# A list scheduler of an FFN: transfer times from the trace, due times for PSUM copies, accumulators joined later, and the first plain down burst taken into the list

## Chip, core and metric

The kernel runs on one core of one Trainium2 chip. The metric is device time in microseconds: the median of three runs of the kernel before is 1355.8 us (1353.67 to 1356.29). Float32 goes in and comes out.

## What is computed

One layer of a hybrid decoder: sequence 1024, width 1024, FFN width 2816. The attention and short-convolution half comes first; the change touches the FFN half only.

```python
D_MODEL = 1024; SEQ = 1024; D_FF = 2816; FFN_CONV_K = 3
...
        merged = jax.nn.sigmoid(g_att) * y_att + jax.nn.sigmoid(g_conv) * y_conv
        x = x + rms_norm(merged @ w_out[l], norm_mix_post[l])

        h = rms_norm(x, norm_ffn_pre[l])
        u = causal_dwconv(h @ w_up[l], conv_ffn_w[l])
        a, g = jnp.split(u, 2, axis=-1)
        f = (jax.nn.gelu(g, approximate=True) * a) @ w_down[l]
        x = x + rms_norm(f, norm_ffn_post[l])
```

## The kernel before

Every float32 operand is scaled and split into two float16 halves, and three float16 products stand for one float32 product. The scale needs the operand's sum of squares: ACT squares and sums each tile (`jk_u`, `jk_dn`, `jk_f`), DVE reduces the sums and writes them as `rb_...`, a matmul of one column with ones (`pr_...`) totals them over the partitions, and DVE makes the scale (`sc_u`, `sp_dn`, `sp_f`). ACT then writes the high half and DVE the low one (`wh_u`, `wdh`, `f16`, and `fa`, `fy`, `fs`, `fx`, `wq` for the quads).

The FFN's 22 chunks of 128 rows (`f` = 0 to 21) come in groups of 4, 4, 4, 4, 3 and 3. A chunk has an up projection of seven products of 12 matmuls, a Strassen scheme over two 512-column halves, which go to three PSUM banks `pu{f}a`, `b` and `c` in the order a, b, c, a, b, c, b. After each product its bank is copied or added out: by ACT to `cg`, `ug` and `ca`, by DVE to `ca` and `cg`. Then come the convolution (`ua`, `ug`), the gelu and the product `ua`. The chunk's weights are two tiles of 512 KB (`ws_u{f}_0`, `_1`) that SP loads.

The first four groups go through the down projection as quads: seven Strassen products of four tiles each, 28 steps of 6 matmuls (`pq`). ACT copies each bank out, scaled, to `st`, and POOL sends every two copies by DMA to a DRAM accumulator `acc[i, e]`, 512 KB: a plain write for the first group, an accumulating DMA for the other three. Beside the last chunks the accumulators are joined (`join`): SP loads them to `yacc` and `u2`, POOL accumulates two more on top, and DVE adds `u2` to three halves of every `yacc` pair. The last two groups are plain: `down` multiplies the split `f16` and `wdh`, and DVE adds `pd` to `yacc`. For the fifth group this runs behind the list, and `dn_split` loads its `w_down` tiles and those of the sixth a second time (`wd`), because the list has only taken their sums of squares.

All up to the last chunk is given to a list scheduler, `Plan`. `add` notes a job with its engine, its cost in us, the tiles it reads and writes, how far it may run ahead of its latest start (`ahead`), and by when it should be done (`due`, reckoned on the clock of the PE jobs). PE products are a fixed sequence (`seq`); other jobs are taken by time and latest start, and a `pr` matmul is put in at once when the list has its operand ready. `order` counts buffers of the pools (16 slots of 4 KB per partition, 4 `ws`, 8 `wh`, 8 PSUM banks) and one DMA queue: a transfer starts when the last one ends. The jobs' code is then emitted in that order, which fixes each engine's instruction order; the chip's engines run these in order and wait on semaphores.

Lines: 1426 `load`, 1450 the `pr` matmul, 1462 and 1464 the two halves, 1537 the up products, 1543 to 1555 their copies, 1697 the quad matmuls, 1701 the `st` copies, 1727 the adds of `join`, 1333 the reloads, 1367 the plain down matmuls.

Of the kernel before, what the change touches and what calls it, by code (L numbers as in the profile page):

```python
# [40 lines left out]
class Layer:  # L41
# [1270 lines left out]
    def ffn(self):  # L1312
# [88 lines left out]
        C = dict(A=0.97, Ah=0.5, Aq=1.18, V=1.21, Vh=0.64, Vp=0.72)  # L1401
# [24 lines left out]
        def load(eng, b, dst, srcf, mb=1.3, r=(), w=None, **kw):  # L1426
            e = nc.sync if eng == "SP" else nc.gpsimd
            j = pl.add(eng, 0.45 if eng == "SP" else 1.1, lambda: e.dma_start(dst(), srcf(), **kw), r,  # L1428
                       [b] if w is None else w, ahead=1e9 if kw or r else AHEAD["load"])
# [187 lines left out]
        def w_sums(g):  # L1617
# [117 lines left out]

        ET = mybir.EngineType
        with tc.manual_schedule(engines={ET.PE, ET.DVE, ET.Activation, ET.SP, ET.Pool}):
# [4 lines left out]
            for f in range(NFF):  # L1742
                g = max(g for g in range(ng) if ff0[g] <= f)
                n = f - ff0[g]
                if f >= 2:
                    up_open(f)
                    up_prod(f, 1)
                if f >= 1 and not (n == 2 and 1 <= g <= NQ):
                    up_prod(f - 1, 4)
                    up_done(f - 1)  # L1750
                if n == 0 and 1 <= g <= NQ:
                    f_quads(g - 1)
                if n == 1 and g == NQ + 1:
                    f_plain(g - 1)
                up_prod(f, 6)
                if f >= 2:
                    up_prod(f, 5)
                    up_prod(f, 2)
                up_prod(f, 7)
                up_prod(f, 3)  # L1760
                if f + 3 < NFF:
                    up_weights(f + 3)
                if n == 1 and 1 <= g <= NQ:
                    quad_open(g - 1)
                    for k, i in enumerate((1, 2, 5, 3, 7, 4, 6)):
                        quad_prod(g - 1, i)
# [3 lines left out]
                if n == 1 and g < NQ:  # L1770
                    w_quads(g)
                if n == 1 and g >= NQ:
                    w_sums(g)
                if g == NQ and n == 2:
                    for tt in range(4):
                        join(tt)
# [2 lines left out]
        for g in (ng - 2,):
            f16[g] = [b.t for b in up[f"q{g}"].f]  # L1780
            invd[g] = fb[g].t["inv"]
        for g in (ng - 2, ng - 1):
            draw[g] = sqs[g].t
        fts[ng - 1] = [up[ff0[ng - 1] + n].ua.t for n in range(GROUPS[ng - 1] - 1)]
# [2 lines left out]
        p, pr = up[NFF - 1], prs[NFF - 1]
        pr.ca, pr.cg, pr.ug, pr.ps = p.ca.t, p.cg.t, p.ug.t, {"b": p.bank["b"].t}
        pr.ua = p.ua.t
        pr.inv = p.sb.t["inv"]  # L1790
        self.pw[f"u{NFF - 1}"] = [b.t for b in p.w], pr.inv
# [396 lines left out]
```

## Time and profile before

| | |
|---|---|
| median of 3 runs | 1355.8 us (1353.67 to 1356.29) |
| the profiled execution | 1353.56 us |
| its span, first to last instruction | 1351.8 us |
| granted TensorE clock, mean | 0.991 |
| bytes moved by DMA | 126.55 MB |

The page gives busy time for each engine over the span, then the span in 40 slices of 33.8 us. PE is the matmul row, PEld the loading of weights beside it, SPq the queue from which SP issues DMAs. In a row of the timeline stand start, length, engine, line, operation, what it writes and reads, how many were merged, and in brackets the idle time before it with what ended that. A row of the waits gives the waiting instruction, what it waited for, us in total, times, and the longest. Names in the profile leave the numbers of buffers out, so `pr_u` stands for `pr_u3` to `pr_u21`.

### The profile page before, as it was taken

To read this page: it belongs to the slowest core of one execution; us is meant where nothing else is said; L and a number is where in the kernel's file an instruction comes from. 1 tells how busy PE (TensorE), PEld (TensorE's weight loads), DVE (VectorE), ACT (ScalarE), POOL (GpSimd) and SP (SyncE) were. 2 spreads that over 40 slices of the span, in tenths; PEclk is the share of its full clock that TensorE was granted. 3 is DMA by queue.
4 is the path that set the end of the run, shared out by engine and by line. 5 is a ranking of instruction groups with operands and counts; after the bars stand their busy time and mean duration, and the time that the engine had idled before them with its cause. 6 is when DMAs were issued, how large, how long until landed. Compare 5 with 4: busy or idle time off the path is not lost.

```text
span 1351.8 us, 17009 instructions
## 1 busy us (share of the span) xinstructions
PE 1302.7 (96%) x6406; PEld 582.3 (43%) x6406; DVE 1095.4 (81%) x1761; ACT 942.0 (70%) x1338; POOL 85.7 (6%) x122
## 2 busy tenths in 40 slices
PE   8999999999999999999999999999899889969997
PEld 4444444444444444444544444444344334324443
DVE  6678988887889867887899999799499669748986
ACT  7578878887788947665576769777677766647625
POOL 2000000000000000000110001002100300130003
PEclk9999999999999999999999999999999999989999
DMA  7111111110112113422420315405911941697117
GB/s 267 33 33 47 48 32 32 48 32 17 47 32 73 39 61 109 157 77 94 145 73 32 125 32 211 162 32 101 241 63 32 213 129 33 137 286 200 57 37 125
DMA packets 36981, 126.55 MB, mean 94 GB/s; under 512 B 4241, under 2 KB 4369, under 8 KB 36898
## 3 DMA queue, kind: packets, MB, share of 16 engines
q1 hardware_dynamic: 26240, 88.76, 19.5%
q0 software_dynamic: 10656, 36.70, 13.0%
q8 instruction: 50, 0.82, 0.2%
q14 instruction: 33, 0.27, 0.1%
q10 hardware_dynamic: 2, 0.00, 0.0%
HBM read 87.67 MB, written 37.78 MB: 93 GB/s over the span
## 4 chain that ended last, share of the span: by engine, by line
PE 49%; issue 25%; DVE 11%; DMA 6%; ACT 5%; POOL 4%; POOLq 0%; DVEq 0%; SPq 0%; ACTq 0%
PE py L1180 5%; PE pcb L212 3%; PE pcc L212 3%; PE pcx L212 3%; PE pk L212 3%; PE pq L212 3%; PE pywa L806 3%; PE pywc L806 3%; DMA ws_u<-w_up_nt 3%; PE pd L1367 3%; POOL acc L1428 2%; PE A L834 2%; PE o L834 2%; PE z L834 2%; PE pv L407 1%
## 5 line engine op out<-in xcount | busy, mean ns | idle before, releaser
L1537 PEld LDWEIGHTS <-wh_u 128*128 128x128 f16 x1764 | 172.0, 98 | 216.2 <-issue 13.1
L1464 DVE SCALAR_TENSOR_TENSOR wh_u<-ws_u,sc_u,wh_u 128x1024 f16<-128x1024 f32 (+1 forms) x60 | 65.6, 1104 | 28.0 <-ACT wh_u L1462 27.7
L2058 PEld LDWEIGHTS <-wh_g 128*128 128x128 f16 x588 | 56.9, 98 | 69.0 <-issue 0.8
L1701 ACT ACTIVATE st<-pq,sd 128x512 f32<-128x512 f32 x112 | 70.0, 686 | 19.9 <-DVE ua L1582 13.3
L1180 PE MATMUL py<-wh_wo,m 128*128 128x512 f16 x384 | 83.7, 379 | 0.0
L877 ACT ACTIVATE sh<-sp 128x1024 f16<-128x1024 f32 (+3 forms) x48 | 40.5, 843 | 52.2 <-DVE sp L872 52.0
L1428 POOL DMA_DIRECT2D acc<-st x56 | 43.4, 774 | 466.9 <-ACT st L1701 466.9
L59 ACT ACTIVATE jk_u<-ws_u 128x1024 bf16<-128x1024 f32 x44 | 46.2, 1051 | 35.0 <-DMA ws_u<-w_up_nt 34.8
L1367 PE MATMUL pd<-wdh,f 128*128 128x512 f16 (+1 forms) x297 | 62.4, 372 | 0.6 <-ACT wdh L98 0.6
L1462 ACT ACTIVATE wh_u<-ws_u,sc_u 128x1024 f16<-128x1024 f32 (+1 forms) x60 | 59.3, 998 | 3.8 <-DVE sc_u L1447 3.5
L872 DVE TENSOR_TENSOR sp<-A,sp 1x1024 f32<-1x1024 f32 (+3 forms) x40 | 35.9, 897 | 29.8 <-PE A L834 26.5
L881 DVE TENSOR_TENSOR sh<-sp,sh 128x1024 f16<-128x1024 f32 (+3 forms) x48 | 45.8, 955 | 13.5 <-ACT sh L877 13.3
L1180 PEld LDWEIGHTS <-m 128*128 128x128 f16 x384 | 37.4, 98 | 44.2
L1571 DVE SCALAR_TENSOR_TENSOR ua<-ca,cw_a,ua 128x1023 f32<-128x1023 f32 (+1 forms) x40 | 51.1, 1278 | 1.1 <-ACT ua L1569 1.1
L907 DVE SCALAR_TENSOR_TENSOR w<-e,w 128x1024 f16<-128x1024 f32 (+3 forms) x48 | 45.8, 954 | 6.8 <-ACT w L903 6.7
L903 ACT ACTIVATE w<-e 128x1024 f16<-128x1024 f32 (+3 forms) x48 | 40.5, 844 | 14.7 <-DVE e L898 13.7
L1697 PE MATMUL pq<-wq,fs 128*128 128x512 f16 x192 | 44.6, 389 | 5.0 <-ACT st L1701 4.7
L1571 DVE SCALAR_TENSOR_TENSOR ug<-cg,cw_g,ug 128x1023 f32<-128x1023 f32 (+1 forms) x38 | 48.6, 1278 | 0.0
L898 DVE TENSOR_TENSOR e<-e,g 128x1024 f32<-128x1024 f32 (+3 forms) x48 | 45.7, 952 | 2.5 <-ACT g L894 2.5
L867 ACT ACTIVATE sp<-e,one 128x1024 f32<-128x1024 f32 (+3 forms) x48 | 44.4, 926 | 4.0 <-DVE e L862 2.7
L853 ACT ACTIVATE e<-z,cz 128x1024 f32<-128x1024 f32 (+3 forms) x48 | 43.1, 898 | 3.6 <-PE z L834 3.6
L212 PE MATMUL pcb<-hT,wh_cb 128*128 128x512 f16 x192 | 45.1, 380 | 0.0
(766 smaller groups left out, 3042.3 us busy)
## 6 DMA issues: line engine op xcount, KB each, us to landing
acc<-st POOLq DMA_DIRECT2D x56, 512.0 KB, 8.5
ws_u<-w_up_nt SPq DMA_DIRECT2D x44, 512.0 KB
ds<-w_down SPq DMA_DIRECT2D x22, 512.0 KB
ws_g<-w_in_nt SPq DMA_DIRECT2D x14, 512.0 KB
x<-x SPq DMA_DIRECT2D x8, 512.0 KB
ws_wo<-w_out SPq DMA_DIRECT2D x8, 512.0 KB
xr<-x SPq DMA_DIRECT2D x8, 512.0 KB
yacc<-acc SPq DMA_DIRECT2D x16, 256.0 KB
```

The lines of the kernel that those rows point to most:

```text
L212: nc.tensor.matmul(ps, w[:, wi, ds(k * P, P)], hT[:, hi, k, ds(c * NH, NH)], start=n == 0, stop=n == last)
L806: nc.tensor.matmul(ps, w[0][:, wi, ds((d % 2) * NH + k * P, P)], acts[bi][k][:, hi, ds(c * NH, NH)], start=n == 0, stop=n == 11)
L834: nc.tensor.matmul(out, w, mv, skip_group_check=True, **kw)
L1180: nc.tensor.matmul(ps, m16[k][:, hi, ds(tt * P, P)], wo[k][:, wi, sl], start=k == 0 and p == 0, stop=k == 7 and p == 2)
L1367: nc.tensor.matmul(pd[nh], f16[g][k][:, hi, ds(tt * P, P)], w[k][:, wi, ds(*part)], start=run is runs[0] and n == 0, stop=run is runs[-1] ...
L1428: j = pl.add(eng, 0.45 if eng == "SP" else 1.1, lambda: e.dma_start(dst(), srcf(), **kw), r, [b] if w is None else w, ahead=1e9 if kw or r ...
L1462: A(C["A" if big else "Ah"], lambda: act.activation(dst.t[:, 0, dsl], src.t[:, ssl], AF.Copy, scale=sb.t["s"]), [(src, sreg), sb], [(dst, ...
L1464: V(C["V" if big else "Vh"], lambda: vec.scalar_tensor_tensor(dst.t[:, 1, dsl], src.t[:, ssl], sb.t["s"], dst.t[:, 0, dsl], ALU.mult, ALU. ...
L1537: pe.matmul(b.t, p.w[wt].t[:, wi, ds(wc * NH + k * P, P)], pr.block(i, h, k), start=first and n == 0, stop=n == 3 * KH - 1, skip_group_che ...
L1571: V(C["V"], lambda lag=lag: vec.scalar_tensor_tensor(u.t[:, lag:], c.t[:, :T - lag], sm.t[:, 2 - lag:3 - lag], u.t[:, lag:], ALU.mult, ALU ...
L1701: A(C["Ah"], lambda tt=tt, b=b, st=st: act.activation(st.t[:, tt % 2, :], b.t, AF.Copy, scale=q.sd.t[:, 0:1]), [b, q.sd], [(st, str(tt % 2))])
L2058: nc.tensor.matmul(ps, w[wt][:, wi, ds(wc * NH + k * P, P)], self.block(i, hi, k), start=first and n == 0, stop=n == 3 * KH - 1, skip_grou ...
```

## The change

Seven things are edited, all in the FFN's list: the costs of ACT's split (`As`, `Ash`) get entries of their own; loads are reckoned longer, and start 1.9 us (SP) or 2.4 us (POOL) after their issue; accumulating DMAs count 2.7 us; the `st` copies and the down copies get a due time of 3 us behind their products; the loads of `join` may run only 20 us ahead of need, where they had no limit, and `u2` is loaded and accumulated for two tiles at once; the raw `w_down` tiles of the sixth group stay in `ws` buffers and are split in the list; and the first plain down burst (`down_plain`), with the end of the last chunk, is in the list too, in place of `dn_split`, `finish` and `down` behind it. The loop over the chunks becomes a generator (`steps`), whose option to interleave products (`inter`) is left at zero.

```diff
-        C = dict(A=0.97, Ah=0.5, Aq=1.18, V=1.21, Vh=0.64, Vp=0.72)
+        C = dict(A=0.97, Ah=0.5, As=1.04, Ash=0.6, Aq=1.18, V=1.21, Vh=0.64, Vp=0.72)
...
-        def load(eng, b, dst, srcf, mb=1.3, r=(), w=None, **kw):
+        def load(eng, b, dst, srcf, mb=1.45, r=(), w=None, ahead=None, **kw):
...
-            j = pl.add(eng, 0.45 if eng == "SP" else 1.1, lambda: e.dma_start(dst(), srcf(), **kw), r,
-                       [b] if w is None else w, ahead=1e9 if kw or r else AHEAD["load"])
+            j = pl.add(eng, 0.45 if eng == "SP" else 1.14, lambda: e.dma_start(dst(), srcf(), **kw), r,
+                       [b] if w is None else w, ahead=AHEAD["load"] if ahead is None else ahead)
...
-        AHEAD = dict(load=45.0, sq=40.0, up=32.0, quad=40.0, wq=60.0)
+        AHEAD = dict(load=45.0, sq=40.0, up=32.0, quad=40.0, wq=60.0, wp=40.0, join=20.0, pr=3.0, cv=1.0, ca=1.0, mb=2.7)
...
-        DUE = dict(conv=20.0, fin=25.0)
+        DUE = dict(conv=20.0, fin=25.0, ev=3.0)
...
-                b = slab(f"ds{ff0[g] + n}")
+                b = slab(f"ds{ff0[g] + n}") if g < ng - 1 else \
+                    Buf("ws", lambda n=n: self.ws.tile([P, D], F32, tag="ws", name=f"ds{ff0[g] + n}"))
...
-                  [b, q.sd], [(st, str(tt % 2))])
+                  [b, q.sd], [(st, str(tt % 2))], due=DUE["ev"])
...
-                    load("G", None, lambda e=tt // 2: acc[i, e], lambda st=st: st.t, r=[st], w=[accb[i, tt // 2]], mb=1.6, **kw)
+                    load("G", None, lambda e=tt // 2: acc[i, e], lambda st=st: st.t, r=[st], w=[accb[i, tt // 2]], mb=AHEAD["mb"], ahead=1e9, **kw)
...
-            u = slab(f"u2_{tt}", [P, NH])
+            if tt % 2 == 0:
+                us[tt // 2] = slab(f"u2_{tt}", [P, 2, NH])
+            u = us[tt // 2]
...
-                load(eng, None, lambda: b.t[:, sl], lambda: m(i), r=[accb[i, tt // 2]], w=[(b, reg)], mb=0.65, **kw)
-            ld("SP", u, slice(0, NH), None, 1)
+                load(eng, None, lambda: b.t[:, sl], lambda: m(i), r=[accb[i, tt // 2]], w=[(b, reg)], mb=1.35 if kw else 0.72, ahead=AHEAD["join"], **kw)
+            if tt % 2 == 0:
+                load("SP", u, lambda: u.t, lambda: acc[1, tt // 2], r=[accb[1, tt // 2]], ahead=AHEAD["join"])
...
+        def down_plain(g):
+            q, w = up[f"q{g}"], up[f"w{g}"]
...
+            for tt in range(8):
+                pd = [Buf("pm", lambda tt=tt, nh=nh: self.bank(f"pd{g}_{tt}_{nh}")) for nh in range(2)]
...
+                        pl.add("PE", 0.2165 * len(run), mm, q.f + w.w, [pd[nh]], seq=True)
+                for nh in range(2):
+                    sl = ds(nh * NH, NH)
+                    V(C["Vp"], lambda b=pd[nh], y=yb_[tt], sl=sl: vec.scalar_tensor_tensor(
+                        y.t[:, sl], b.t, sd.t[:, 0:1], y.t[:, sl], ALU.mult, ALU.add), [pd[nh], sd], [(yb_[tt], "lh"[nh])], due=DUE["ev"])
...
-            conv(NFF - 1, up[NFF - 1].ua, up[NFF - 1].ca, NFF - 1, "a")
+            up_prod(NFF - 1, 4)
+            up_done(NFF - 1)
+            down_plain(ng - 2)
+            f_plain(ng - 1)
             pl.emit()
...
-        dn_split(ng - 2)
-        prs[NFF - 1].prod(4)
-        finish(NFF - 1)
-        dn_split(ng - 1, True)
-        down(ng - 2, lambda tt: tt == 5 and f_split(ng - 1))
         down(ng - 1)
...
             if e in ("SP", "G"):
-                dma = max(dma, t + 0.8) + j.load
-                done = max(done, dma + 1.2)
+                dma = max(dma, t + (1.9 if e == "SP" else 2.4)) + j.load
+                done = dma + 0.5
```

The numbers move instructions in many places. Three of them matter below. The first is the end of the second burst, as chunk 10 begins. On ACT, before, where `st1_4` and `st1_6` are the last quad copies, `jk_u12` the square sums of chunk 12's weights, and `cg10` the copy of the first product of chunk 10:

```order
L1701 ACTIVATE st1_4_2_8631<-pq1_3_7_8573,sd1_8239 128x512
L59 ACTIVATE jk_u12_0_8649,sm_u12_8648<-ws_u12_0_8608 128x1024
L1701 ACTIVATE st1_6_0_8658<-pq1_0_6_8634,sd1_8239 128x512
L59 ACTIVATE jk_u12_1_8669,sm_u12_8648<-ws_u12_1_8619 128x1024
L1701 ACTIVATE st1_6_0_8658<-pq1_1_6_8651,sd1_8239 128x512
L1701 ACTIVATE st1_6_2_8684<-pq1_2_6_8662,sd1_8239 128x512
L1701 ACTIVATE st1_6_2_8684<-pq1_3_6_8672,sd1_8239 128x512
L1546 ACTIVATE cg10_8722<-pu10a_8687 128x512
```

On ACT, with the change, at the same place:

```order
L1702 ACTIVATE st1_6_0_8647<-pq1_0_6_8625,sd1_8231 128x512
L1702 ACTIVATE st1_6_0_8647<-pq1_1_6_8639,sd1_8231 128x512
L1702 ACTIVATE st1_6_2_8669<-pq1_2_6_8650,sd1_8231 128x512
L59 ACTIVATE jk_u12_0_8676,sm_u12_8675<-ws_u12_0_8604 128x1024
L1702 ACTIVATE st1_6_2_8669<-pq1_3_6_8660,sd1_8231 128x512
L1546 ACTIVATE cg10_8706<-pu10a_8678 128x512
L59 ACTIVATE jk_u12_1_8708,sm_u12_8675<-ws_u12_1_8620 128x1024
L1550 ACTIVATE ug10_8749<-pu10c_8713 128x512
```

The square sums move behind three copies each. On PE, before, `pr_u12` stands behind the first product of chunk 10 (`pu10a`) and ahead of the second (`pu10b` with `wh_u10_2`):

```order
L1537 LDWEIGHTS wh_u10_0_8548
L1537 MATMUL pu10a_8687<-hA_5680,wh_u10_0_8548 128x512
L1450 LDWEIGHTS ones_84
L1450 MATMUL pr_u12_8705<-rb_u12_8681,ones_84 128x1
L1537 LDWEIGHTS wh_u10_2_8567
L1537 MATMUL pu10b_8709<-hB2_5681,wh_u10_2_8567 128x512
```

With the change it stands behind the fourth product (the second `pu10a`) and ahead of the fifth (`pu10b` with `wh_u10_1`):

```order
L1537 LDWEIGHTS wh_u10_0_8519
L1537 MATMUL pu10a_8678<-hA_5680,wh_u10_0_8519 128x512
L1450 LDWEIGHTS ones_84
L1450 MATMUL pr_u12_8756<-rb_u12_8727,ones_84 128x1
L1537 LDWEIGHTS wh_u10_1_8581
L1537 MATMUL pu10b_8693<-hB2_5681,wh_u10_1_8581 128x512
```

So it moves three products later; in the next burst `pr_u16` moves from behind the second product of chunk 14 to behind the fourth, in the last `pr_u20` from behind the third of chunk 18 to behind the fourth. The second place is SP's queue in the last burst. Before, behind `ws_u19` and two loads of `u2`:

```order
L1428 DMA yacc0_10333<-acc2_0_6605 128x512
L1428 DMA u2_2_10335<-acc1_1_6604 128x512
L1428 DMA u2_3_10357<-acc1_1_6604 128x512
L1428 DMA yacc1_10398<-acc2_0_6605 128x512
L1428 DMA yacc0_10333<-acc3_0_6607 128x512
L1428 DMA yacc1_10398<-acc3_0_6607 128x512
L1428 DMA yacc2_10456<-acc3_1_6608 128x512
L1428 DMA yacc3_10465<-acc3_1_6608 128x512
L1428 DMA yacc2_10456<-acc2_1_6606 128x512
L1428 DMA yacc3_10465<-acc2_1_6606 128x512
L1428 DMA ws_u20_0_10496<-w_up_nt 128x1024
L1428 DMA ws_u20_1_10505<-w_up_nt 128x1024
```

With the change, from `ws_u19` on:

```order
L1428 DMA ws_u19_1_10141<-w_up_nt 128x1024
L1428 DMA ws_u20_0_10470<-w_up_nt 128x1024
L1428 DMA ws_u20_1_10483<-w_up_nt 128x1024
L1428 DMA ds16_10609<-w_down 128x1024
L1428 DMA ds17_10613<-w_down 128x1024
L1428 DMA ds18_10632<-w_down 128x1024
L1428 DMA ws_u21_0_10638<-w_up_nt 128x1024
L1428 DMA ws_u21_1_10643<-w_up_nt 128x1024
L1428 DMA ds19_10865<-w_down 128x1024
L1428 DMA ds20_10886<-w_down 128x1024
L1428 DMA u2_0_10932<-acc1_0_6603 128x1024
L1428 DMA ds21_10953<-w_down 128x1024
```

All loads of accumulators stand behind the last weights of the up projection. The third place is DVE around the last chunk. Before:

```order
L1727 TENSOR_TENSOR yacc2_10456<-yacc2_10456,u2_2_10335 128x512
L1571 SCALAR_TENSOR_TENSOR ug20_10950<-cg20_10895,cw_g20_10662,ug20_10950 128x1022
L1727 TENSOR_TENSOR yacc6_10577<-yacc6_10577,u2_2_10335 128x512 x2
L1727 TENSOR_TENSOR yacc3_10465<-yacc3_10465,u2_3_10357 128x512
L1582 TENSOR_TENSOR ua20_11021<-ug20_10950,ua20_11021 128x1024
L1727 TENSOR_TENSOR yacc7_10580<-yacc7_10580,u2_3_10357 128x512 x2
L1543 TENSOR_TENSOR cg21_11036<-pu21b_11040,cg21_11036 128x512
```

With the change:

```order
L1733 TENSOR_TENSOR yacc2_11036<-yacc2_11036,u2_2_11000 128x512
L1567 TENSOR_SCALAR cw_a21_11099<-cfw_91,sc_u21_10725,g_ffn_5689 128x3
L1582 TENSOR_TENSOR ua20_11020<-ug20_10927,ua20_11020 128x1024
L1733 TENSOR_TENSOR yacc3_11061<-yacc3_11061,u2_2_11000 128x512
L1440 TENSOR_REDUCE sp_dn5_11120<-sm_dn5_10905 128x1
L1441 CAST rb_dn5_11121<-sp_dn5_11120 128x1
L1543 TENSOR_TENSOR cg21_11016<-pu21b_11022,cg21_11016 128x512
L1733 TENSOR_TENSOR yacc4_11064<-yacc4_11064,u2_0_10932 128x512
L1555 TENSOR_TENSOR cg21_11016<-cg21_11016,ug21_11079 128x512
L1543 TENSOR_TENSOR ca21_11058<-pu21c_11043,ca21_11058 128x512
```

Where all twelve adds stood ahead of this `cg21`, the second of the last chunk's sums on DVE, eight now stand behind it, among the chain to `f16` of the sixth group, and `rb_dn5` comes behind the adds of `yacc2` and `yacc3`.

More of the change, by code (lines that the diff above doesn't have):

```diff
@@ L1723, in join @@
             ld("SP", y, hi, "h", 3)
-            ld("G", u, slice(0, NH), None, 6, accum_op=ALU.add)
+            if tt % 2 == 0:
+                load("G", u, lambda: u.t, lambda: acc[6, tt // 2], r=[accb[6, tt // 2]], ahead=AHEAD["join"], mb=2.7,
+                     accum_op=ALU.add)
             ld("G", z, hi, "h", 5, accum_op=ALU.add)
             for b, sl, reg in ((y, hi, "h"), (z, lo, "l"), (z, hi, "h")):
-                V(C["Vh"], lambda b=b, sl=sl: vec.tensor_tensor(b.t[:, sl], b.t[:, sl], u.t, ALU.add), [u], [(b, reg)])
+                V(C["Vh"], lambda b=b, sl=sl: vec.tensor_tensor(b.t[:, sl], b.t[:, sl], u.t[:, tt % 2], ALU.add), [u], [(b, reg)])
         def f_plain(g):
@@ L1741, in ffn, with steps @@
                 up_open(f)
[L1742 to L1766, printed above, removed]
+            def steps():
+                for f in range(NFF):
+                    g = max(g for g in range(ng) if ff0[g] <= f)
+                    n = f - ff0[g]
+                    if f >= 2:
+                        up_open(f)
+                        up_prod(f, 1)
+                        yield
+                    if f >= 1 and not (n == 2 and 1 <= g <= NQ):
+                        up_prod(f - 1, 4)
+                        up_done(f - 1)
+                    if n == 0 and 1 <= g <= NQ:
+                        f_quads(g - 1)
+                    if n == 1 and g == NQ + 1:
+                        f_plain(g - 1)
+                    for i in (6, 5, 2, 7, 3):
+                        if f >= 2 or i not in (5, 2):
+                            up_prod(f, i)
+                            if i != 3:
+                                yield
+                    if f + 3 < NFF:
+                        up_weights(f + 3)
+                    if n == 1 and 1 <= g <= NQ:
+                        quads.append((g - 1, f))
+                    if n == 1 and g < NQ:
+                        w_quads(g)
+                    if n == 1 and g >= NQ:
+                        w_plain(g)
+                    if g == NQ and n == 2:
+                        for tt in range(4):
+                            join(tt)
+                    yield
@@ L1767, in ffn @@
+            quads = []
+            st = steps()
+            for _ in st:
+                while quads:
+                    g, f = quads.pop()
+                    quad_open(g)
+                    for k, i in enumerate(MORDER):
+                        quad_prod(g, i)
                         if k == 0:
@@ L1769, in ffn @@
                             up_done(f)
[L1770 to L1776, printed above, removed]
-            conv(NFF - 1, up[NFF - 1].ua, up[NFF - 1].ca, NFF - 1, "a")
-            pl.emit()
[L1779 to L1784, printed above, removed]
+                        for _ in range(INTER[k]):
+                            next(st)
+            up_prod(NFF - 1, 4)
+            up_done(NFF - 1)
+            down_plain(ng - 2)
+            f_plain(ng - 1)
+            pl.emit()
+        g = ng - 1
+        f16[g], invd[g] = [b.t for b in up[f"q{g}"].f], fb[g].t["inv"]
+        draw[g] = [b.t for b in up[f"w{g}"].w], up[f"w{g}"].sb.t["inv"]
         for tt in range(8):
             yacc[tt] = yb_[tt].t
[L1787 to L1791, printed above, removed]
-        dn_split(ng - 2)
-        prs[NFF - 1].prod(4)
-        finish(NFF - 1)
-        dn_split(ng - 1, True)
-        down(ng - 2, lambda tt: tt == 5 and f_split(ng - 1))
         down(ng - 1)
```

35 lines of the change are left out of this document (28 added, 7 removed).

## The prediction

> **What bounds the kernel now.** I read the page's engine table first, then the PE row of the slices, then PE's waits from 690 us on, then the timeline of PE at the points where a burst of quad products begins.
>
> ```profile
> PE 1302.7 (96%) x6406; PEld 582.3 (43%) x6406; DVE 1095.4 (81%) x1761; ACT 942.0 (70%) x1338; POOL 85.7 (6%) x122
> PE   8999999999999999999999999999899889969997
> PE pr_u L1450 <- DVE rb_u L1441: 15.3, 3, 10.0
> PE pq L1697 <- ACT st L1701: 5.8, 5, 3.0
> PE pr_u L1450 <- ACT st L1701: 3.3, 1, 3.3
> ```
>
> TensorE is the bound. The matmuls are the same before and after (the built programs have equally many PE rows), so only idle time and slow matmuls can go. But for the first, the slices below 9 stand after 946 us (a slice is 33.8). There PE waits above all for `pr_u`, the tiny matmul that totals the squares of a weight chunk; it needs the chunk's two DMAs, and stands in PE's queue ahead of products that don't need it yet.
>
> The FFN repeats one cycle: a burst of 28 quad products (6 matmuls each) and 28 up products (12 each). These rows are the first quad products of the four bursts, and the first product of the down projection:
>
> ```profile
> 803.97 2.32 PE L1697 MATMUL pq<-wq,fa 128*128 128x512 f16 x10
> 913.03 5.34 PE L1697 MATMUL pq<-wq,fa 128*128 128x512 f16 x24
> 1030.34 5.34 PE L1697 MATMUL pq<-wq,fa 128*128 128x512 f16 x24
> 1147.88 3.40 PE L1697 MATMUL pq<-wq,fa 128*128 128x512 f16 x15
> 1279.74 19.59 PE L1367 MATMUL pd<-wdh,f 128*128 128x512 f16 x90 [0.62 <-ACT wdh L98]
> ```
>
> The first cycle takes 109.06 us, the next 117.31 and 117.54, the last stretch 131.86. In the first, PE has no gap. The last stretch has 29 up products, one more, and one takes 2.59 us from start to start:
>
> ```profile
> 800.00:850.00 50.00, 50.00 (x236) 22.62 (x234) 44.25 (x71) 41.86 (x60) 7.51 (x14) 1.00 0.49 185
> 850.00:900.00 50.00, 50.00 (x235) 22.68 (x234) 43.80 (x62) 36.51 (x50) 0.00 (x0) 1.00 0.26 89
> 1263.37 2.75 PE L1537 MATMUL pu21b<-hB,wh_u 128*128 128x512 f16 x12
> 1265.96 2.75 PE L1537 MATMUL pu21c<-hB,wh_u 128*128 128x512 f16 x12
> ```
>
> Against 109.06 the losses are **8.25, 8.48 and 20.21, together 36.9 us**. That is all there is to win here: from 1279.74 to the last product PE waits for nothing that the table of waits shows.
>
> What sets the first burst apart is how its results leave: plain DMA writes, where later bursts accumulate in DRAM. The columns of these windows are length, busy time of PE, PEld, DVE, ACT, POOL, granted clock, DMA share, GB/s.
>
> ```profile
> 840.00:850.00 10.00, 10.00 (x49) 4.58 (x48) 6.01 (x14) 7.38 (x14) 1.60 (x3) 1.00 1.02 395
> 940.00:950.00 10.00, 9.93 (x48) 4.45 (x47) 9.06 (x18) 9.81 (x14) 2.56 (x3) 1.00 1.06 211
> 980.00:1030.00 50.00, 50.00 (x235) 22.73 (x234) 49.65 (x72) 36.31 (x48) 0.00 (x0) 1.00 0.13 43
> ```
>
> With all DMA engines busy in both, 395 GB/s move when plain and 211 when accumulating: 512 KB take 1.33 and 2.48 us. The list reckoned 1.6 for either. The burst whose transfers it reckoned long enough has no gap; the bursts it reckoned too short have 8 us each.
>
> **The change part by part.** *Transfer times.* The list now reckons 2.7 us for an accumulate, 1.45 for a weight load, and 1.9 us ahead of each on SP (before 0.8). What that must mend, at chunk 12:
>
> ```profile
> 948.01 1.81 SPq L1428 DMA_DIRECT2D ws_u<-w_up_nt  x2
> 953.85 2.75 PE L1537 MATMUL pu10a<-hA,wh_u 128*128 128x512 f16 x12
> 955.85 1.06 ACT L59 ACTIVATE jk_u<-ws_u 128x1024 bf16<-128x1024 f32 x1 [3.61 <-DMA ws_u<-w_up_nt]
> 959.67 1.06 ACT L59 ACTIVATE jk_u<-ws_u 128x1024 bf16<-128x1024 f32 x1 [2.09 <-DMA ws_u<-w_up_nt]
> 961.34 0.18 PE L1450 MATMUL pr_u<-rb_u,ones 128*128 128x1 bf16 x1 [4.74 <-DVE rb_u L1441]
> 962.43 0.60 ACT L1546 ACTIVATE cg<-pu10a 128x512 f32<-128x512 f32 x1
> ```
>
> The weights are issued at 948.0, used by ACT at 955.9 and 959.7, and PE stands 4.74 us. ACT is in order too: the copy of `pu10a` out of PSUM runs only at 962.43, though that product was done before 957. In the changed order `pr_u12` stands three up products later (3 x 2.59 = 7.8 us, more than 4.74), and `pr_u16` two (5.2 against its 3.29). On ACT three of the last four quad copies now stand ahead of the first square sum, and the fourth and the copy of `pu10a` ahead of the second. So both waits should go, with 3.0 and 1.9 us to spare; what is late next is the copy `ug10`, needed only a product later. The four `w_down` loads, issued from 952.97 on in the same traffic, now come after that point.
>
> *Accumulators joined later.* In the last burst, SP has twelve loads of accumulators to issue, each waiting for its last accumulate, ahead of `ws_u20`:
>
> ```profile
> 1175.54 14.95 SPq L1428 DMA_DIRECT2D yacc<-acc  x7
> 1190.59 0.94 SPq L1428 DMA_DIRECT2D ws_u<-w_up_nt  x2
> 1207.35 1.06 ACT L59 ACTIVATE jk_u<-ws_u 128x1024 bf16<-128x1024 f32 x1 [12.90 <-DMA ws_u<-w_up_nt]
> 1211.14 0.18 PE L1450 MATMUL pr_u<-rb_u,ones 128*128 128x1 bf16 x1 [10.02 <-DVE rb_u L1441]
> 1211.19 5.28 PE L1537 MATMUL pu18a<-hA,wh_u 128*128 128x512 f16 x12
> ```
>
> `ws_u20` goes out 42.7 us after its burst's start (1190.59 less 1147.88), `ws_u12` 35.0 after its own; then it competes with the joins and lands after 17 us, not 8. Now it is next in SP's queue after `ws_u19`, and no join stands ahead of `ws_u21`. Landing like `ws_u12` (ready 48.3 us after the burst's start, 961.34 less 913.03), it meets `pr_u20` behind 28 quad and five up products: 36.3 + 13.0 = 49.3 us. So the 10.02 us go, and the slow matmuls behind them, 5.28 where twelve take 2.75.
>
> *Deadlines for PSUM copies* aim at `pq <- st`:
>
> ```profile
> 1169.13 3.39 PE L1697 MATMUL pq<-wq,fs 128*128 128x512 f16 x8 [2.96 <-ACT st L1701]
> 1078.82 2.75 PE L1537 MATMUL pu14c<-hB,wh_u 128*128 128x512 f16 x12
> ```
>
> All five such waits are 5.8 us, with 0.3 for `fs`, and the eight matmuls behind the longest took 3.39 us where 8 x 0.216 = 1.7 was due: 7.8 together. A copy can be early only if a slot for its result is free, and slots stay held until the slow accumulates land; bounds 0 and 7.8, and I keep **half, 3.9**. The Trainium skill ("TensorE: Matmul & The Clock Gate", "What's actually happening") halves the clock only after an idle window of about 3.4 us. The trace disagrees at 1169 (2.96 us of waiting, slow matmuls) and agrees at 1078.8, where 3.29 us were followed by full speed; by the rule the 1.7 would not come back, and the sum would be 0.9 lower.
>
> *The down burst in the list.* Six reloads of `w_down` and their issues on SP go, three megabytes; the squares, splits and down products stay as many.
>
> ```profile
> 1238.56 45.95 SPq L1333 DMA_DIRECT2D wd<-w_down  x6
> 1305.06 1.27 DVE L99 SCALAR_TENSOR_TENSOR f<-ua,sc,f 128x1024 f16<-128x1024 f32 x1
> ```
>
> PE waits 0.62 us there now, and DVE has the last split of the second burst done at 1306.3, 4.6 us before PE needs it (1279.74 plus 144 products of 0.2165, 1310.9). So at most 0.62 is to be won, and I count nothing. What it may cost: eight `yacc` adds of 0.6 us come into this stretch, three splits of 1.2 leave it, and the spare falls to some 3.4 us. With the adds gone behind `ca21` and `cg21` a late accumulate stops DVE, and behind it `rb_dn5`, `cg21` and the chain to `pr_f5`, which stand in PE's queue.
>
> ```profile
> acc<-st POOLq DMA_DIRECT2D x56, 512.0 KB, 8.5
> yacc<-acc POOLq DMA_DIRECT2D x4, 256.0 KB, 15.3
> u<-acc POOLq DMA_DIRECT2D x4, 256.0 KB, 17.2
> ```
>
> The list reckons 5.6 us from issue to landing (2.4 + 2.7 + 0.5); the trace has 8.5 for quad accumulates, and 17.2 for joins amid other traffic. The wait is thus 0 to 11.6 us; I take **2.9**, by the row with the most transfers. Two loads and two accumulates of `u2` in place of four of each move the same bytes; POOL is 6% busy: nothing. The other entries (`As`, `Ash`, 1.14 for POOL, `w_quads` called ahead of a burst, settings kept at their old values) add no instruction and move ACT and DVE work by a place or two; DVE works 95 us of a 117 us cycle (row below) and ACT less, so they have room: nothing.
>
> The **sum**: the profiled execution took 1353.6 us (span 1351.8 and 1.8 around it). Less 36.9 is 1316.7; 3.9 and 2.9 back make 1323.5. The median of the runs lies 2.2 above that execution; I lean half a microsecond up and say 1324.
>
> **The rivals.** *New waits at the joins* (1335). The price is the upper end: 1316.7 + 3.9 + 11.6, and 2.5 for slow matmuls as at 1211.19. For it: DVE runs its queue in order, and all twelve adds stand late in it. Against it: the 17 us were measured while weight loads, joins and accumulates were all queued at once. The Trainium skill ("DMA: Bandwidth & Descriptors", "Issuing engines are not separate DMA queues") says that DMAs of all issuers interleave on the same 16 engines. By that rule SP's accumulator loads slow POOL's accumulates, which the list reckons in one file one after the other; it gives this rival's time, and the 17.2 agrees with it.
>
> *The waits stay, on another engine* (1343). DVE is busy 49.65 of 50 us between bursts (the window at 980 above). If it can't keep up, PE, released from `pr_u`, waits for a split or for a bank that DVE has not emptied: the second and third cycles keep their 16.7 us and the last keeps half of its 20.2, 1353.6 - 10.1 = 1343.5. Against it:
>
> ```profile
> 913.03:1030.34 117.31, 111.14 (x511) 49.66 (x510) 95.18 (x144) 83.51 (x116) 11.95 (x14) 0.99 0.49 117
> ```
>
> Over a whole cycle DVE works 95.2 us, less than the 109 of matmuls.
>
> *It doesn't do what it says* (1354): the square sums move, but the weights land later by as much. For that the landing after issue would have to grow from 7.8 us to over 15; DMA is 0.49 busy over the cycle. *Slower*: the six accumulates of the joins land one after another, 2 x 17.2 + 4 x 15.3 = 95.6 us. Beside the 31.2 us of the down burst 64 us of waiting would be left, 1388; it turns slower than before once the six take over 61 us. Against it:
>
> ```profile
> 1210.05 1.96 POOL L1428 DMA_DIRECT2D yacc<-acc  x2
> 1217.96 1.74 POOL L1428 DMA_DIRECT2D u<-acc  x2 [2.43 <-DMA acc<-st]
> DMA to landing us min/median/max: 9.8/15.3/20.5
> ```
>
> Eight such accumulates, issued between these two, landed within 20.5 us at most (the `yacc` ones), so they overlap.
>
> **How the numbers follow.** The forecast, 1315 to 1331, gets 0.69; its low end is all 36.9 gone and a little more. Waits at the joins (1331 to 1340) 0.13, waits on DVE (1340 to 1350) 0.09, no effect 0.04, slower 0.05. The range of 1315 to 1340 takes in the first two. Faster by over 0.2% (about 2.7 us, what a measurement of this kernel can tell from no change) has 0.91, within it 0.04, slower 0.05.
>
> **What would show it.** In the changed profile: no wait of PE for `rb_u` over 2 us, where there were three with 15.3 together; first quad products 109 to 112 us apart; a granted clock of 1.00 from 950 to 1270; ACT's `ug`, `cg` and `st` copies no longer behind `jk_u`; no `wd` issues at L1333, and joins issued only after the last `ws_u`. PE's idle time should fall from 49 us to some 25. I am wrong in the main step if they stay 117 us apart; wrong in the end if PE waits over 5 us for `rb_dn5` or `rb_f5`, or if DVE's adds wait for accumulates over 10 us together.

## The result, and the profile after

| | before | after |
|---|---|---|
| median | 1354.74 us (4 runs, 1353.67 to 1356.29) | 1319.5 us (4 runs, 1318.67 to 1320.99) |
| ratio, with its 95% interval | | 0.974 (0.9723 to 0.9757) |
| the profiled execution, and its span | 1353.56, 1351.8 | 1320.99, 1319.3 |
| granted clock, mean | 0.991 | 0.998 |

The forecast was 1324 with a range of 1315 to 1340: sign, size and range hold, and the time is 4.5 us below the point. The first view of the changed kernel is the page's engine table, with the slices of PE (a slice is now 33.0 us):

```profile
PE 1294.4 (98%) x6406; PEld 581.3 (44%) x6406; DVE 1097.4 (83%) x1761; ACT 941.7 (71%) x1338; POOL 83.6 (6%) x120
PE   8999999999999999999998999999999999999997
```

PE has the same 6406 matmuls. Its busy time fell by 8.3 us, though the work is the same: those were matmuls at a lower clock. Its idle time, span less busy, fell from 49.1 to 24.9 us. The run of slices below 9 after 946 us is gone. Second view, of PE's waits from 690 us on the longest and what is left of `pr_u`:

```profile
PE pq L1698 <- ACT st L1702: 3.9, 4, 1.8
PE pr_u L1450 <- DVE rb_u L1441: 0.3, 1, 0.3
```

Of 15.3 us of waits for `rb_u` 0.3 are left; the 3.3 in which `pr_u` waited behind `st` are gone. Third view, the timeline of PE: the first quad products of the four bursts and the first product of the down projection.

```profile
803.64 4.70 PE L1698 MATMUL pq<-wq,fa 128*128 128x512 f16 x21
912.57 5.34 PE L1698 MATMUL pq<-wq,fa 128*128 128x512 f16 x24
1021.88 5.34 PE L1698 MATMUL pq<-wq,fa 128*128 128x512 f16 x24
1133.00 5.34 PE L1698 MATMUL pq<-wq,fa 128*128 128x512 f16 x24
1247.31 17.64 PE L1766 MATMUL pd<-wdh,f 128*128 128x512 f16 x81
```

The cycles take 108.93, 109.31 and 111.12 us and the last stretch 114.31, where they took 109.06, 117.31, 117.54 and 131.86. From the first down product to the end of the span it is 72.1 and 72.0 us (1351.8 less 1279.74, 1319.3 less 1247.31). So the gain lies where it was looked for: against 109.06 and 111.65, cycles 2 and 3 and the last stretch now lose 0.25, 2.06 and 2.66, together 5.0 us of the former 36.9.

Around chunk 12, which is shown before, the rows of SP, ACT and PE are now:

```profile
947.28 0.99 SPq L1428 DMA_DIRECT2D ws_u<-w_up_nt  x2
952.83 1.06 ACT L59 ACTIVATE jk_u<-ws_u 128x1024 bf16<-128x1024 f32 x1
954.64 0.60 ACT L1546 ACTIVATE cg<-pu10a 128x512 f32<-128x512 f32 x1
956.33 1.06 ACT L59 ACTIVATE jk_u<-ws_u 128x1024 bf16<-128x1024 f32 x1 [1.09 <-DMA ws_u<-w_up_nt]
959.62 2.75 PE L1537 MATMUL pu10a<-hA,wh_u 128*128 128x512 f16 x12
962.21 0.17 PE L1450 MATMUL pr_u<-rb_u,ones 128*128 128x1 bf16 x1
```

`pr_u` runs at 962.21 without a wait, 49.6 us after its burst's start; before it ran at 961.34, 48.3 after, with 4.74 us of waiting. It does not run earlier: what changed is that three more products stand ahead of it. ACT copies `pu10a` at 954.64 instead of 962.43, and waits 1.09 us where it waited 3.61 and 2.09. Part of that is an earlier landing: the second square sum begins 43.8 us after the burst's start, where it was 46.6.

The four waits for `st` stand at two points:

```profile
1041.85 5.34 PE L1698 MATMUL pq<-wq,fs 128*128 128x512 f16 x24 [1.67 <-ACT st L1702]
1052.59 4.04 PE L1698 MATMUL pq<-wq,fy 128*128 128x512 f16 x18 [0.22 <-ACT st L1702]
1153.06 5.34 PE L1698 MATMUL pq<-wq,fs 128*128 128x512 f16 x24 [1.76 <-ACT st L1702]
1163.81 4.04 PE L1698 MATMUL pq<-wq,fy 128*128 128x512 f16 x18 [0.23 <-ACT st L1702]
```

They are 1.89 us in cycle 3 and 1.99 in the last stretch: 3.88 of the 4.72 us that these still lose. SP's queue in the last burst, and the DMA issues with their median from issue to landing:

```profile
1169.22 0.99 SPq L1428 DMA_DIRECT2D ws_u<-w_up_nt  x2
1170.31 5.91 SPq L1428 DMA_DIRECT2D ds<-w_down  x3
1186.26 1.30 SPq L1428 DMA_DIRECT2D ws_u<-w_up_nt  x2
1215.81 0.33 SPq L1428 DMA_DIRECT2D u<-acc  x1
1223.01 1.48 SPq L1428 DMA_DIRECT2D yacc<-acc  x3
```

```profile
acc<-st POOLq DMA_DIRECT2D x56, 512.0 KB, 7.0
u<-acc POOLq DMA_DIRECT2D x2, 512.0 KB, 7.1
yacc<-acc POOLq DMA_DIRECT2D x4, 256.0 KB, 5.2
```

`ws_u20` goes out 36.2 us after the burst's start (42.7 before), the joins only behind the last `ws_u`, and the joins' accumulates land in 7.1 us (`u2`, now 512 KB each) and 5.2 us (`yacc`) where they took 17.2 and 15.3.

### The profile page after: what moved, and what is told of

It reads as the page before. It is cut to its first block, busy times and chain, and to the rows that moved or that the text cites. A ratio compares the mean times of both kernels' runs of the same rounds, so it can differ in the third digit from the quotient of the medians.

```text
span 1319.3 us, 16991 instructions
## 1 busy us (share of the span) xinstructions
PE 1294.4 (98%) x6406; PEld 581.3 (44%) x6406; DVE 1097.4 (83%) x1761; ACT 941.7 (71%) x1338; POOL 83.6 (6%) x120
## 3 DMA queue, kind: packets, MB, share of 16 engines
q1 hardware_dynamic: 25088, 85.61, 18.9%
q0 software_dynamic: 10368, 36.70, 13.7%
## 4 chain that ended last, share of the span: by engine, by line
PE 65%; issue 24%; DVE 4%; POOL 3%; ACT 1%; DMA 1%; POOLq 0%; DVEq 0%; ACTq 0%
PE py L1180 5%; PE pcb L212 3%; PE pcc L212 3%; PE pcx L212 3%; PE pk L212 3%; PE pq L212 3%; PE pywa L806 3%; PE pywc L806 3%; POOL acc L1428 3%; PE pd L1766 2%; PE A L834 2%; PE o L834 2%; PE pd L1367 2%; PE z L834 2%; PE pv L407 1%
## 5 line engine op out<-in xcount | busy, mean ns | idle before, releaser
L881 DVE TENSOR_TENSOR sh<-sp,sh 128x1024 f16<-128x1024 f32 (+3 forms) x48 | 45.8, 954 | 13.5 <-ACT sh L877 13.3
L903 ACT ACTIVATE w<-e 128x1024 f16<-128x1024 f32 (+3 forms) x48 | 40.5, 843 | 14.7 <-DVE e L898 13.7
L212 PE MATMUL pcx<-hT,wh_cx 128*128 128x512 f16 x192 | 44.9, 379 | 0.0
```

Source lines behind the costliest of these rows:

```text
L212: nc.tensor.matmul(ps, w[:, wi, ds(k * P, P)], hT[:, hi, k, ds(c * NH, NH)], start=n == 0, stop=n == last)
```

## The experiments

Twelve kernels. Five are the kernel before with one thing done (names with b): three with a part of the change, one with only PE's place altered, one without the suspected cause. Seven are the change with a part undone or altered (a). Each edit is small, but moves instructions in the whole list. So the length of each cycle is read beside the total; with no waits a cycle is some 109.0 us and the last stretch some 111.65. Ratios are to runs of the kernel before on the same chip, with 95% intervals; the lengths are of the profiled execution.

| kernel | median us | ratio | cycles 1, 2, 3 | last stretch |
|---|---|---|---|---|
| before | 1354.74 | | 109.06, 117.31, 117.54 | 131.86 |
| after | 1319.5 | 0.974 (0.9723 to 0.9757) | 108.93, 109.31, 111.12 | 114.31 |
| b_plain | 1324.38, one run | | 109.05, 108.93, 108.93 | 121.23 |
| b_times | 1334.06 | 0.9861 (0.9846 to 0.9876) | 108.93, 114.33, 109.62 | 126.34 |
| b_join | 1339.88 | 0.9911 (0.9895 to 0.9927) | 109.06, 118.66, 119.49 | 118.52 |
| b_ev | 1346.56 | 0.9952 (0.9939 to 0.9966) | 108.93, 113.13, 111.83 | 135.15 |
| b_prlag | 1348.23 | 0.9965 (0.9954 to 0.9977) | 111.01, 114.28, 115.95 | 132.34 |
| a_mb16 | 1323.93 | 0.9789 (0.9769 to 0.9809) | 108.96, 112.62, 108.93 | 120.47 |
| a_oldtimes | 1330.52 | 0.9841 (0.9825 to 0.9856) | 108.93, 114.25, 112.20 | 120.80 |
| a_join1e9 | 1328.88 | 0.9815 (0.9799 to 0.9832) | 108.93, 109.35, 111.22 | 123.96 |
| a_noev | 1319.43 | 0.975 (0.9735 to 0.9764) | 108.93, 108.93, 110.08 | 112.56 |
| a_downout | 1320.61 | 0.9757 (0.9744 to 0.977) | 108.93, 110.26, 109.27 | 113.57 |
| a_noev25 | 1321.29 | 0.9763 (0.9743 to 0.9783) | 108.93, 110.85, 109.68 | 111.55 |
| a_inter | 1341.3 | 0.991 (0.9896 to 0.9923) | 114.96, 114.98, 114.42 | 119.13 |

**b_plain: is the accumulate the cause?** In the kernel before, all quad results leave as plain writes; the sums over the groups are left out. The order of the instructions stays.

```diff
-                    kw = {} if g == 0 else dict(accum_op=ALU.add)
+                    kw = {}
```

> The kernel before with every quad result written plainly to its accumulator (the sums over groups are left out, the order of all instructions stays). If the accumulates' length is the cause, the second and third cycles fall to 109-111 us like the first, with no waits for pr_u, and the last stretch to 112-120. If the order by itself is bad, they stay near 117.

The starts of the bursts, and the median from issue to landing of the quads' DMAs:

```profile
911.64 2.54 PE L1697 MATMUL pq<-wq,fa 128*128 128x512 f16 x11
1020.57 2.75 PE L1697 MATMUL pq<-wq,fa 128*128 128x512 f16 x12
1129.50 1.67 PE L1697 MATMUL pq<-wq,fa 128*128 128x512 f16 x7
acc<-st POOLq DMA_DIRECT2D x56, 512.0 KB, 3.8
PE pu19b L1537 <- DVE ca L1543: 5.6, 1, 5.6
```

Cycles 2 and 3 take 108.93 us, as the first. With the old order untouched, both 8 us losses hang on the longer accumulates (landing 3.8 us against 8.5). The last stretch keeps 9.6 of its 20.2 us, above all as a wait of 5.6 for DVE's `ca` (last row, of the waits) and 2.5 in the slow products behind it: about half of what was lost there has another cause. In the trace the wait goes back over DVE and ACT to the squares of `w_down` tiles (`jk_dn`), for which ACT stands 0.9 to 5.0 us a time; SP issues these tiles only among its loads of accumulators, from 1174.33 on. That points at the joins; b_join tries them.

**b_times, b_join, b_ev: one part alone, in the kernel before.** The new transfer numbers only; the joins' limit of 20 us only; the due time of the `st` copies only.

```diff
-                dma = max(dma, t + 0.8) + j.load
-                done = max(done, dma + 1.2)
+                dma = max(dma, t + (1.9 if e == "SP" else 2.4)) + j.load
+                done = dma + 0.5
...
-                load(eng, None, lambda: b.t[:, sl], lambda: m(i), r=[accb[i, tt // 2]], w=[(b, reg)], mb=0.65, **kw)
+                load(eng, None, lambda: b.t[:, sl], lambda: m(i), r=[accb[i, tt // 2]], w=[(b, reg)], mb=0.65, ahead=20.0, **kw)
...
-                  [b, q.sd], [(st, str(tt % 2))])
+                  [b, q.sd], [(st, str(tt % 2))], due=3.0)
```

(b_times also has `mb` of 1.45, 1.14, 2.7 and 0.72 or 1.35, as the change has them.)

> The kernel before, with only the transfer times of the change in the list (2.7 us per accumulate, 1.45 per load, 1.9 and 2.4 us ahead, 0.5 behind). Theory A (the list reckoned the accumulates too short, and PE and ACT stood behind square sums of weights that had not landed): the second and third cycles fall from 117.3 and 117.5 us to 109 to 112, as with the change (109.3 and 111.1); the last stretch keeps some of its loss, since joins may still go out early: 1353.6 to 1330-1338. Theory B (the deadlines for the PSUM copies, which bring st and cg ahead of jk_u, do it): the two cycles stay near 117, total above 1345.

> The kernel before with only the joins' loads held to 20 us ahead of need. If the joins ahead of ws_u20 cost what the last stretch shows (10.0 us of waiting, some 3 of slow matmuls), the last stretch falls from 131.9 to 117-121 us and the second and third stay at 117: 1338 to 1344. If the late weights of chunk 20 were due to the accumulates alone, it stays over 1350.

> The kernel before with only the due time of 3 us for the st copies. The run with old transfer times (cycles of 114.3 and 112.2 us against 117.3 and 117.5) suggests that due times and transfer times stand in for each other: then this kernel's second and third cycles fall to 112-115 and the last stretch stays at 130-133: 1343 to 1349. If the due times do nothing by themselves either, it stays at 1351 to 1355.

Of PE's waits after 690 us in b_times, b_join and b_ev, in this order, rows for `pr_u` and `st`:

```profile
PE pq L1697 <- ACT st L1701: 5.2, 6, 2.5
PE pr_u L1450 <- DVE rb_u L1441: 2.2, 1, 2.2
...
PE pr_u L1450 <- ACT st L1701: 6.5, 2, 3.4
PE pr_u L1450 <- DVE rb_u L1441: 6.0, 2, 5.3
...
PE pq L1697 <- ACT st L1701: 6.6, 5, 2.4
PE pr_u L1450 <- DVE rb_u L1441: 5.1, 1, 5.1
```

True times are worth 18.9 us (1353.0 less 1334.06), 10.9 of them in cycles 2 and 3 (117.31 + 117.54 less 114.33 and 109.62). Cycle 3 falls as expected; cycle 2 keeps 5.3 us, more than the 109 to 112 that were expected. The later joins are worth 12.9 (1352.8 less 1339.88), and all of that lies in the last stretch, 13.3 us shorter; cycles 2 and 3 keep their waits of `pr_u`. The two together, 31.8, come near the whole gain. The due time alone is worth 6.6 us; it shortens cycles 2 and 3 by 9.9 and lengthens the last stretch by 3.3, just over what was expected there (130 to 133 us, and 135.15 came). The waits for `st`, at which due times aim, are not shorter: 6.6 us where they were 5.8. What fell are the waits of `pr_u`, from 18.6 to 7.0 (5.1 as shown, and 1.9 behind `st`).

**b_prlag: only PE's place.** The list puts each `pr` in 12 us behind its operand, not 3, and nothing else of its numbers is touched.

```diff
-            V(0.3, pre, [smb], [rb]).lag = 3.0
+            V(0.3, pre, [smb], [rb]).lag = 12.0
```

> The kernel before with one number changed: the list puts each pr matmul at least 12 us behind its operand instead of 3. If PE's place in its own queue is what costs, the 18.6 us of waits for pr_u go and the cycles fall to 109-112: 1325 to 1338. If ACT's order behind the DMA (the copies of st, cg and ug behind jk_u) costs as much, PE waits for those copies instead and the cycles stay over 113: 1340 to 1352.

PE's waits, and of ACT's timeline in cycle 3 the square sums ahead of the copy of `pu14a`:

```profile
PE pu18a L1537 <- ACT cg L1546: 5.3, 1, 5.3
PE pu14a L1537 <- ACT cg L1546: 5.2, 1, 5.2
PE pu10a L1537 <- ACT cg L1546: 3.7, 1, 3.7
...
1071.18 1.06 ACT L59 ACTIVATE jk_u<-ws_u 128x1024 bf16<-128x1024 f32 x1 [5.03 <-DMA ws_u<-w_up_nt]
1074.97 1.06 ACT L59 ACTIVATE jk_u<-ws_u 128x1024 bf16<-128x1024 f32 x1 [2.07 <-DMA ws_u<-w_up_nt]
1078.79 1.06 ACT L59 ACTIVATE jk_dn<-ds 128x1024 bf16<-128x1024 f32 x1 [2.67 <-DMA ds<-w_down]
1080.42 0.59 ACT L1546 ACTIVATE cg<-pu14a 128x512 f32<-128x512 f32 x1
```

No long wait for `rb_u` is left, yet only 4.6 us are won: late loads, two of `ws_u` and one of `w_down`, now hold ACT, whose copy of `pu14a` stands behind them, and PE waits for the bank. The wait has to go out of both queues, and true transfer times do that at once.

**a_mb16 and a_oldtimes: the change without true times.** In the first only the accumulate of the quads is reckoned 1.6 us again; in the second all old transfer numbers are back.

```diff
-        AHEAD = dict(..., mb=2.7)
+        AHEAD = dict(..., mb=1.6)
```

> The changed kernel with one number put back: an accumulating DMA is reckoned at 1.6 us instead of 2.7. Theory A: pr_u waits come back in the bursts that accumulate; each of three bursts loses 3 to 8 us more: 1328 to 1340. Theory B: no more than 2 us of difference, 1318 to 1322.

> The changed kernel with all transfer times of before (1.6 and 1.3 and 0.65 us, 0.8 us ahead, 1.2 behind); joins late, due times and the down burst in the list stay. Theory A2 (the transfer times as a whole, loads' latency included, carry the second and third cycles): those cycles lose 5 to 8 us each again, with waits for pr_u, 1333 to 1340. Rival (only the accumulate's number counts): like the run with 1.6 alone, 1322 to 1326.

a_mb16 loses 4.4 us to the change and a_oldtimes 11.0 (by the ratios, which compare runs on one chip, 6.6 and 13.7). Both miss their expectations: 1323.93 lies between the two that were named for a_mb16, 1330.52 between those for a_oldtimes, whose cycles 2 and 3 lose 5.2 and 3.1 us and not 5 to 8 each. The lengths of a_mb16 are those of its slowest execution, 1328.6 us. So the accumulate's number alone is worth less than all transfer numbers together; which of the others does the rest (latency, length of loads, those of the joins) was not tried one by one. With the old times, the other parts of the change still win 22.3 us (1352.8 less 1330.52).

**a_join1e9: the change with the joins as early as before.**

```diff
-        AHEAD = dict(..., join=20.0, ...)
+        AHEAD = dict(..., join=1e9, ...)
```

> The changed kernel with the joins free to run as early as they can, as before. Theory A plus the join term: SP issues accumulator loads ahead of ws_u20 again and PE waits 5 to 13 us for pr_u20 (slow matmuls included), 1325 to 1333; the cycles before the last stay at 109 and 111. Rival (the late joins don't matter once the list knows the transfer times, since SP then places ws_u20 first): 1318 to 1322.

The loss of 9.4 us is as large as expected, but it isn't the wait for `pr_u20`. SP's queue, then one wait of DVE and two of PE in the last stretch:

```profile
1153.13 12.54 SPq L1428 DMA_DIRECT2D yacc<-acc  x4
1170.32 0.33 SPq L1428 DMA_DIRECT2D ws_u<-w_up_nt  x1
...
1196.65 1.31 SPq L1428 DMA_DIRECT2D ws_u<-w_up_nt  x2
...
1216.00 0.69 DVE L1469 TENSOR_TENSOR s_u<-ws_u 128x512 f32<-128x512 f32 x1 [5.98 <-DMA ws_u<-w_up_nt]
...
1217.01 0.16 PE L1450 MATMUL pr_dn<-rb_dn,ones 128*128 128x1 bf16 x1 [2.69 <-DVE rb_dn L1441]
1218.20 5.28 PE L1537 MATMUL pu19b<-hA,wh_u 128*128 128x512 f16 x12 [1.03 <-DVE cg L1543]
```

With true times the list keeps `ws_u20` early although the joins stand around it: 37.2 us after the burst's start (1170.32 less 1133.09). The first `ws_u` row is of chunk 20, the second of chunk 21: with sixteen loads of accumulators ahead of it in this stretch, `ws_u21` goes out 63.6 us after the burst's start (1196.65 less 1133.09), where the changed kernel issues it 53.3 after (1186.26 less 1133.00). DVE stands 5.98 us for it, and `rb_dn` and the sum `cg`, for which PE waits, stand behind it in DVE's queue. So part of the cost is the same as in the kernel before, one chunk later and in another engine's queue. PE waits 8.8 us in seven places of this stretch: 3.4 for `st`, 1.7 for `fx`, and the two shown. The matmuls behind the last wait take 5.28 us, 2.5 too long. These 11.3 are most of the 12.3 that the stretch loses, where the changed kernel loses 2.7. What makes the waits for `st` and `fx` was not tried.

**a_noev and a_noev25: the due times.** `ev` is set to 1e9, so the copies have none; in the second kernel an accumulate is also reckoned 2.5 us, not 2.7.

```diff
-        DUE = dict(conv=20.0, fin=25.0, ev=3.0)
+        DUE = dict(conv=20.0, fin=25.0, ev=1e9)
```

> The changed kernel without due times for the st copies and the down copies. Theory A: the due times are worth at most the 3.9 us of PE waits for st that half remained: 1319 to 1324. Theory B: the main gain goes, over 1335.

> The changed kernel without due times for the copies and with an accumulate reckoned at 2.5 us, as the trace has it (2.48), in place of 2.7. If the plan's numbers are as good as they need be: 1317 to 1321. If the order reacts to a tenth of a microsecond: a cycle loses 3 us or more, over 1322.

a_noev takes as long as the change, and its waits for `st` are even shorter:

```profile
PE pq L1698 <- ACT st L1702: 0.9, 4, 0.4
```

Its cycles lose 3.2 us less than those of the changed kernel in the profiled executions, which its median doesn't show (the runs of each spread over 2 to 4 us). So the due times win nothing that can be measured beside true transfer times, though 6.6 us without them: either shortens the waits of `pr_u`. a_noev25 is no faster, and falls between its two expectations: two tenths of a microsecond in a table (2.7 to 2.5) move a cycle by 0.4 to 1.9 us, either way.

**a_downout: the first plain down burst behind the list again**, with its six reloads of `w_down`, as before.

> The changed kernel with the first plain down burst behind the list again, as before (w_down of the last two groups is loaded a second time). If that part is worth nothing, as forecast: 1317 to 1322. If the reloads beside the late joins hold up the down burst: over 1324, with a wait of PE for wdh.

1320.61 against 1319.5, with ratios whose intervals overlap: this part of the change is worth nothing that can be measured (by the ratios 2.3 us, which the intervals don't tell from none).

**a_inter: the quad products spread among the up products**, by the option that the change adds and leaves at zero (and without the due times).

```diff
-    ahead_set, due_set, inter = {}, {}, (0, 0, 0, 0, 0, 0, 0)
+    ahead_set, due_set, inter = {}, {}, (0, 1, 1, 1, 1, 1, 1)
```

> The changed kernel without due times for the copies, with an up product of the next chunk between the quad products (inter 0,1,1,1,1,1,1), so that the accumulates of a burst are spread over 52 us instead of 39. If the remaining 2 to 5 us of lost time come from saturated DMA in the bursts, they go: 1314 to 1318. If the up products, needing their banks and copies in between, make new waits: 1322 to 1340.

```profile
PE pq L1698 <- ACT st L1702: 16.7, 5, 4.8
```

Every cycle takes some 115 us, the first among them, whose writes are plain, and the time lies 1.3 us above the range for new waits. Spreading the transfers doesn't help; PE waits for the copies out of PSUM instead.

## Why the prediction was right

- **36.9 us to win, all between 913 and 1280 us.** Right: 32.0 of them came, and the part behind it took 72.0 us, before 72.1. PE's idle time fell to 24.9 us, "some 25" as forecast.
- **Square sums that stand too early.** Right, and shown from both sides: without the accumulates the old order loses nothing in cycles 2 and 3 (b_plain), and with PE's place alone changed the wait goes over to ACT (b_prlag). At chunk 12 the working gave 3.0 us to spare; `rb_u` was ready at 958.0, 4.2 us before `pr_u` ran. One reading beside it was wrong: the four `w_down` loads do not come later. SP issues them at 948.33, right behind `ws_u12`, where before it did from 952.97 on; the weights landed in time even so.
- **The joins ahead of `ws_u20`.** Right in size: 13.3 us of the last stretch go with this part alone (b_join). The working took `ws_u20` to be ready 48.3 us after the burst's start, with 1.0 to spare; `pr_u20` ran at 52.0 (1185.03 less 1133.00). That it cost 0.31 us only is in part luck: PE had already stood 1.99 us for `st`. a_join1e9 bears out the way that was named, SP's queue, and shows that it reaches further: joins that run early cost 9.4 us even when `ws_u20` isn't late, in part through a late `ws_u21` that holds DVE, and through waits for `st` and `fx` whose cause is open.
- **3.9 us of `pq <- st` kept.** That it is 3.9 is luck. That such waits hang on slow accumulates is borne out: with plain writes (b_plain) none is left. But the half was to be what due times can't mend, and they mend none of it: b_ev has 6.6 us of these waits with due times, a_noev 0.9 without. Why the orders differ in them stays open.
- **2.9 us for late joins.** The one mis-sized term: it measured nothing. No wait for `rb_dn5` or `rb_f5` appears, and DVE waits for no accumulate. The two totals run without idle time:

```profile
1247.29 0.17 PE L1450 MATMUL pr_dn<-rb_dn,ones 128*128 128x1 bf16 x1
1264.79 0.17 PE L1450 MATMUL pr_f<-rb_f,ones 128*128 128x1 bf16 x1
```

  I priced it from accumulates that landed in 8.5 and 17.2 us. The order has room for that: in a_noev the `yacc` ones land in 13.6 us, and PE waits under 1 us for all that follows from them. And here they land sooner. These rows are POOL's first issues of them and the median landing, in the changed kernel and in a_noev:

```profile
1234.88 0.85 POOL L1428 DMA_DIRECT2D yacc<-acc  x1 [3.38 <-DMA yacc<-acc]
...
1232.50 3.71 POOL L1428 DMA_DIRECT2D yacc<-acc  x4
yacc<-acc POOLq DMA_DIRECT2D x4, 256.0 KB, 13.6
```

  Spread over 8 us (the last is issued at 1242.6) they take 5.2, all four within 3.7 us 13.6. The same holds in a_mb16 and a_oldtimes (spread over some 9 us, 5.9 and 5.6) and in a_downout and b_join (within some 4 us, 14.4 and 15.0). It is no rule: in b_times, b_ev and b_prlag the four are issued over 16 to 28 us and take 10.2 to 13.5, amid other accumulates and loads. I carried a duration over from another order, in which POOL issues eight of them within 9.7 us (1210.05 to 1219.70); what made it long there stays open.
- **The 4.5 us below the point**, by terms: 2.9 for the joins; 0.5 that I leaned up for the median; 1.5 as this median lies below its profiled execution; 0.6 from the first cycle and the stretches outside; less the 1.1 by which cycles 2 and 3 and the last stretch kept more than 3.9 (together 4.4).
- **The down burst in the list: nothing.** Right (a_downout).
- **The rivals.** Waits at the joins did not come, though SP's loads of accumulators kept the DMA engines full meanwhile (the window's next to last column is the DMA share):

```profile
1235.00:1245.00 10.00, 10.00 (x48) 4.58 (x47) 9.19 (x15) 3.29 (x5) 3.32 (x4) 1.00 1.06 264
```

  Three of the four `yacc` accumulates are issued in this window and the first just ahead of it; they land in 4.4 to 7.2 us. I had given this rival the rule of the Trainium skill that DMAs of all issuers interleave on the same engines ("DMA: Bandwidth & Descriptors", "Issuing engines are not separate DMA queues"). They may, but full engines alone did not make the accumulates late. DVE did not become the bound: over cycle 3 it works 95.6 of 111.1 us. Weights that land later by as much, and joins that go one after another, both fall by the rows above.

## What to carry to other kernels

Where a list orders the work, look for the stage in which its reckoned times are true and compare it with those where they aren't: the difference of the cycles (here 109 against 117 us) is what truer numbers can win. A tiny operation that waits for a transfer costs every queue that it stands in, so moving it in one alone only hands the wait on. Parts of a change that each win alone (18.9, 12.9 and 6.6 us) need not add up; undo each inside the whole change to see what it is still worth (11.0, 9.4 and nothing that can be measured).

## What the hardware showed

- With all DMA engines busy, accumulating moves 211 GB/s and plain writing 395, in the windows of 10 us shown ahead; the landing of a quad's 512 KB has a median of 3.8 us when all are plain (b_plain), 7.0 and 8.5 in the kernels after and before, where three of four are accumulating. It alone does not set the time: a_noev, as fast as the change, has 8.4.
- The 256 KB accumulates of the joins took from 5.2 to 17.2 us from issue to landing (medians). Four issued within some 5 us took 11.2 us or more in every kernel; spread ones took 5.2 to 5.9 in three kernels and 10.2 to 13.5 in three others. Whether the accumulates delay one another, or other traffic beside them does, was not tried.
- Slow matmuls follow waits of uneven length. After 2.96 us eight ran at about half speed in the kernel before; after 3.34 us in b_times (row below) twelve took their full-speed 2.75; in a_join1e9 two waits of 2.69 and 1.03 us close together were followed by 5.28. The rule of an idle window of about 3.4 us in the Trainium skill ("TensorE: Matmul & The Clock Gate", "What's actually happening") fits the second only. The first shows that a shorter wait can do it, and so does the third: PE stands from 1214.32 on, and the granted clock is 0.58 from 1216.50 to 1217.00 and 0.50 after that, before 3.4 us have passed.

```profile
1197.47 2.75 PE L1537 MATMUL pu18c<-hA,wh_u 128*128 128x512 f16 x12 [3.34 <-ACT ug L1550]
```
